# A two-layer hybrid mixer with experts: layer 1's S5 matrices computed during layer 0's experts

## The chip, the cores and the metric

One core of a Trainium2 chip. The metric is the device time of one execution in microseconds (us); lower is better. Engines are named as in the profile: PE (TensorE), DVE (VectorE), ACT (ScalarE), POOL (GpSimd), SP (SyncE, which here only issues DMAs).

## The reference

Two layers over 512 latent and 256 context tokens of width 1024, all in float32. A layer is a mixer of four branches (attention, SSD, S5, short convolution) merged by sigmoid gates, then experts with expert choice. The parts that matter here:

```python
def s5_discretise(lam_re, lam_im, log_step, b_re, b_im):
    step = jnp.exp(log_step)[:, None]
    mag = jnp.exp(lam_re * step)
    ab_re, ab_im = mag * jnp.cos(lam_im * step), mag * jnp.sin(lam_im * step)
    ...
    return ab_re, ab_im, bb_re, bb_im

h[t] = ab * h[t-1] + bb @ u[t]          # complex, 24 groups, both directions
y = re(c @ h) + d * u                   # then gelu and a gate

aff = softmax(h @ w_router); gval, idx = top_k(aff.T, cap)   # cap = 2*T/16
hid = silu(xg @ w_gate) * (xg @ w_up);  ye = (hid @ w_down) * gval
out = zeros.at[idx].add(ye)             # 16 experts, 64 latent and 32 context rows each
```

Layer 1 needs no context output, so only its latents pass the second half of the mixer and the experts. The S5 parameters do not depend on the tokens: the matrices that S5 needs (`ab`'s powers, `bb`, `c`) can be computed at any time.

## The kernel before

Dense products of the mixer are done as three fp32r matmuls (`mm3`, L98 to L100) with operands split by a cast on ACT (L113) and a subtraction on DVE (L114). Tile's scheduler decides the static order of each engine from the program's order and its priorities; no order is written out by hand.

`branches` (L380) emits SSD, S5 and attention, each with its own PSUM tag (a, b, a), and then `main()`: short convolution and 16 `gate` chunks (L409 to L419), which use PSUM tag mm and are the work that PE takes while a branch has nothing for it. In layer 0 they cover 768 tokens (tiles of 512 and 256 columns), in layer 1 the 512 latents.

`s5` (L1002) projects and transposes u, then makes on DVE the step, the exponentials and sines, the powers `pw`, `un`, `lo`, `hi` and the tables `PB`, `PC` (L1023 to L1116). Then it loops over 6 groups of 4 S5 groups. In each: `Bx` by a complex product on POOL (`cmul`, L995 to L1000, called at L1127), `Cx` by a complex product on DVE (L1128; six operations of 128x640), transposes of Bx to `Bt` (L1134), 16 small matmuls for the kernel `KK` (L1143) with its copies (L1147 to L1149) and 8 DMAs on SP that spread KK to `T0` (L1152); then u's transposes, the copy U on ACT (L1158) and the reversed copies Ur on DVE (L1159, L1160), the drive matmuls (L1165, L1166), T by a complex product on POOL (L1172), the rotation by T on DVE (L1177 to L1182), eight scans (L1185), the rotation back to S (L1192 to L1196), the output matmuls (L1201, L1203) and their sum into u_tok (L1207). All of it uses PSUM tag b with three buffers.

`moe` (L1244) runs 16 experts. Per expert `up` (L1340) does the gate product and then the up product for the latents (64 columns, two parts of 512) and the context (32 columns, four parts of 256); `hidden` (L1351) does tanh on ACT (L1357), two DVE operations (L1358, L1359), transposes on PE (L1362) and the copy hidT on ACT (L1364); `down` (L1367) the down product (L1376), the scaling on DVE (L1381) and an indirect DMA on POOL that adds the rows to DRAM (L1384). Expert weights stream on SP in chunks of 1 MB (`wchunks`, L298) through a rotation of buffers. The residual's SBUF tile `x` is idle in that time; it is reloaded at expert 11 (context) and 13 (latents), L1386 to L1388. In layer 0 nothing ties the latent job's matmuls to the context job's: the scheduler may alternate them.

Of the kernel before, what the change touches and what calls it, by code (L numbers as in the profile page):

```python
# [55 lines left out]
MOE = ((2, 3, 3), (3, 3, 2))  # L56


class Kern:
    def __init__(self, ctx, tc, I, out):  # L60
        self.ctx, self.tc, self.nc, self.I, self.out = ctx, tc, tc.nc, I, out
        self.uid = 0
        self.early, self.wafter = (2, 7), {}
# [81 lines left out]
    def setup(self):  # L145
# [30 lines left out]
        self.gs = [dr(f"gs{b}", 8, 128, 768) for b in range(4)]  # L176

# [823 lines left out]

    def s5(self):  # L1002
# [20 lines left out]
        keep = lambda nm, *s: wp.tile([128, *s], F32, name=nm)  # L1023
        bb = [keep("bbr", 25, 16), keep("bbi", 25, 16)]
        cc = keep("cc", 2, 24, 16)
        s5d = keep("s5d", 384)
        PB, PC = keep("PB", 2, 8, 24), keep("PC", 2, 10, 24)
        rho = keep("rho", 24)
        lo, hi = keep("lo", 2, 17, 24), keep("hi", 2, 6, 24)
        with self.pool("s5p") as pp:  # L1030
            sm = lambda nm, *s: pp.tile([128, *(s or (24,))], F32, name=nm)
            p5 = sm("p5", NPS5 - 384)
            nc.scalar.dma_start(p5, self.I["ps5"][l, :, 384:])
            nc.scalar.dma_start(s5d, self.I["ps5"][l, :, :384])
            pr = {k: p5[:, a - 384:b - 384] for k, (a, b) in _PS5.items()}
            V.tensor_copy(cc[:, 0], v3(pr["cr"]))
            V.tensor_copy(cc[:, 1], v3(pr["ci"]))

            step, mag, ang = sm("step"), sm("mag"), sm("ang")
            nc.scalar.activation(step, pr["ls"], AF.Exp)  # L1040
            V.tensor_mul(mag, pr["lr"], step)
            nc.scalar.activation(mag, mag, AF.Exp)
            V.tensor_mul(ang, pr["li"], step)
            t, sn, cn = sm("t"), sm("sn"), sm("cn")
            M = 12582912.0
            V.tensor_scalar(t, ang, 1.0 / (2 * np.pi), M, op0=OP.mult, op1=OP.add)
            V.tensor_scalar(t, t, M, None, op0=OP.subtract)
            V.scalar_tensor_tensor(ang, t, -6.28125, ang, op0=OP.mult, op1=OP.add)
            V.scalar_tensor_tensor(ang, t, -(2 * np.pi - 6.28125), ang, op0=OP.mult, op1=OP.add)
            V.tensor_scalar(ang, ang, 3.1415925, -3.1415925, op0=OP.min, op1=OP.max)  # L1050
            nc.scalar.activation(sn, ang, AF.Sin)
            nc.scalar.activation(cn, ang, AF.Sin, scale=0.5)
            V.tensor_mul(cn, cn, cn)
            V.tensor_scalar(cn, cn, -2.0, 1.0, op0=OP.mult, op1=OP.add)
            pw = sm("pw", 2, 9, 24)
            x1 = sm("x1", 8, 24)
            V.memset(pw[:, 0, 0], 1.0)
            V.memset(pw[:, 1, 0], 0.0)
            V.tensor_mul(pw[:, 0, 1], mag, cn)
            V.tensor_mul(pw[:, 1, 1], mag, sn)  # L1060

            def powers(P, first, last):

                a = 1
                while a < last:
                    n = min(a, last - a)
                    A = [P[:, i, a:a + 1].to_broadcast([128, n, 24]) for i in range(2)]
                    B = [P[:, i, 1:1 + n] for i in range(2)]
                    self.cmul(V, P[:, 0, a + 1:a + 1 + n], P[:, 1, a + 1:a + 1 + n], *A, *B, x1[:, :n])
                    a *= 2  # L1070

            powers(pw, 1, 8)

            nr, den, cr, ci = sm("nr"), sm("den"), sm("cr"), sm("ci")
            ni = pw[:, 1, 1]
            V.tensor_scalar(nr, pw[:, 0, 1], -1.0, None, op0=OP.add)
            V.tensor_mul(den, pr["lr"], pr["lr"])
            V.tensor_mul(t, pr["li"], pr["li"])
            V.tensor_add(den, den, t)
            V.reciprocal(den, den)  # L1080
            V.tensor_mul(cr, nr, pr["lr"])
            V.tensor_mul(t, ni, pr["li"])
            V.tensor_add(cr, cr, t)
            V.tensor_mul(cr, cr, den)
            V.tensor_mul(ci, ni, pr["lr"])
            V.tensor_mul(t, nr, pr["li"])
            V.tensor_sub(ci, ci, t)
            V.tensor_mul(ci, ci, den)
            bc = lambda a: a[:, :, None].to_broadcast([128, 24, 16])
            for b in bb:  # L1090
                V.memset(b[:, 24], 0.0)
            self.cmul(V, bb[0][:, :24], bb[1][:, :24], bc(cr), bc(ci), v3(pr["br"]), v3(pr["bi"]), sm("y1", 24, 16))

            V.memset(PC, 0.0)
            for s in range(8):
                V.tensor_copy(PB[0:64, :, s], pw[0:64, :, 7 - s])
            V.tensor_copy(PB[64:128], pw[64:128, :, 0:8])
            V.tensor_copy(PC[0:64, :, 0:9], pw[0:64])
            for k in range(9):
                V.tensor_copy(PC[64:128, :, 9 - k], pw[64:128, :, k])  # L1100

            V.tensor_mul(rho, mag, mag)
            V.tensor_mul(rho, rho, rho)
            V.tensor_mul(rho, rho, rho)
            un = sm("un", 2, 9, 24)
            V.tensor_copy(un[:, 0, 1], cn)
            V.tensor_copy(un[:, 1, 1], sn)
            for a in (1, 2, 4):
                A = [un[:, i, a:a + 1] for i in range(2)]
                self.cmul(V, un[:, 0, 2 * a:2 * a + 1], un[:, 1, 2 * a:2 * a + 1], *A, *A, x1[:, :1])  # L1110
            V.memset(hi[:, 0, 0], 1.0)
            V.memset(hi[:, 1, 0], 0.0)
            V.tensor_copy(lo[:, :, 1], un[:, :, 8])
            powers(lo, 1, 16)
            V.tensor_copy(hi[:, :, 1], lo[:, :, 16])
            powers(hi, 1, 5)  # L1116
        with self.pool("s5b") as bp:
            W = lambda nm, *s: bp.tile([128, *s], F32, name=nm)
            for g0 in range(0, 24, 4):
                gg = slice(g0, g0 + 4)  # L1120

                Bx = [W(f"Bx{i}", 4, 8, 16) for i in range(2)]
                Cx = [W(f"Cx{i}", 4, 10, 16) for i in range(2)]
                z1, e1 = W("z1", 4, 10, 16), W("e1", 4, 8, 16)
                ap = lambda P, n, i: P[:, i, :, gg].rearrange("p s g -> p g s")[:, :, :, None].to_broadcast([128, 4, n, 16])
                av = lambda v, n: v[:, gg][:, :, None, :].to_broadcast([128, 4, n, 16])
                self.cmul(nc.gpsimd, Bx[0], Bx[1], ap(PB, 8, 0), ap(PB, 8, 1), av(bb[0], 8), av(bb[1], 8), e1)  # L1127
                self.cmul(V, Cx[0], Cx[1], ap(PC, 10, 0), ap(PC, 10, 1), av(cc[:, 0], 10), av(cc[:, 1], 10), z1)  # L1128
                nc.scalar.mul(Cx[1], Cx[1], -1.0)
                Bt = [W(f"Bt{i}", 4, 128) for i in range(2)]  # L1130
                for i in range(2):
                    ps = self.va(512)
                    for q in range(4):
                        nc.tensor.transpose(ps[:, q * 128:(q + 1) * 128], Bx[i][:, q].rearrange("p s i -> p (s i)"), self.ident)  # L1134
                    nc.scalar.copy(Bt[i].rearrange("p a b -> p (a b)"), ps)

                KK = bp.tile([16, 4, 15, 16], F32, name="KK")
                kf = [self.va(128).rearrange("p (d j) -> p d j", d=8) for _ in range(2)]
# [15 lines left out]
                U, Ur = W("U", 4, 96), W("Ur", 4, 96)  # L1154
                ps = self.va(384).rearrange("p (g b) -> p g b", g=4)
                for q in range(4):
                    nc.tensor.transpose(ps[:, q], u_tok[:, g0 + q].rearrange("p s i -> p (s i)"), self.ident[:96, :96])
# [3 lines left out]
                pv = []  # L1161
                for i in range(2):
                    p = self.va(384).rearrange("p (g b) -> p g b", g=4)
                    for q in range(4):
                        nc.tensor.matmul(p[0:64, q], Bt[i][:, q, 0:64], U[:, q], start=True, stop=True, skip_group_check=True)  # L1165
                        nc.tensor.matmul(p[64:128, q], Bt[i][:, q, 64:128], Ur[:, q], start=True, stop=True, skip_group_check=True)  # L1166
                    pv.append(p)
# [91 lines left out]
    def experts(self, l, mp, slotT, io, m5):  # L1259
# [3 lines left out]
        with self.pool("gat", side="right") as gp, self.pool("exp", side="right") as wp, ExitStack() as es:  # L1263
# [76 lines left out]
            def up(w, X, ps, job, e, side):  # L1340
# [3 lines left out]
                for k in range(8):  # L1344
# [3 lines left out]
                    if k % 4 == 3:  # L1348
                        next(side, None)
# [301 lines left out]
```

## Time and profile before

| | |
|---|---|
| runs (3) | 3120.9 to 3125.51 us, median 3123.74 |
| profiled execution | 3125.83 us, span 3124.1 us, mean granted clock 0.966 |
| PE busy | 2846.2 us (91%) |
| DVE / ACT / POOL busy | 1559.2 / 783.8 / 619.7 us |
| layer 0's S5 | about 360 to 546 us of the span |
| layer 0's experts | 1131.6 to 1732.9 us |
| layer 1's S5 | about 2004 to 2242 us, its gates go on until about 2440 |

The span is one execution as the profiler recorded it; the profiled execution's own time is 1.7 us more. Line numbers are those of the kernel before.

### The profile page before, as it was taken

To read this page: it belongs to the slowest core of one execution; us is meant where nothing else is said; L and a number is where in the kernel's file an instruction comes from. 1 tells how busy PE (TensorE), PEld (TensorE's weight loads), DVE (VectorE), ACT (ScalarE), POOL (GpSimd) and SP (SyncE) were. 2 spreads that over 40 slices of the span, in tenths; PEclk is the share of its full clock that TensorE was granted. 3 is DMA by queue.
4 is the path that set the end of the run, shared out by engine and by line. 5 is a ranking of instruction groups with operands and counts; after the bars stand their busy time and mean duration, and the time that the engine had idled before them with its cause. 6 is when DMAs were issued, how large, how long until landed. Compare 5 with 4: busy or idle time off the path is not lost. (4 is left out here: it accounts for less than half of the span.)

```text
span 3124.1 us, 47057 instructions
## 1 busy us (share of the span) xinstructions
PE 2846.2 (91%) x18626; PEld 1826.3 (58%) x18626; DVE 1559.2 (50%) x3507; ACT 783.8 (25%) x1725; POOL 619.7 (20%) x765
## 2 busy tenths in 40 slices
PE   7999878999999979999999799977999896998887
PEld 4866756788888943433333376756687684332223
DVE  5477688555436552212111546798856565232223
ACT  4253222426522200000000332322436421000001
POOL 1022165120004121111110104065220031010001
PEclk9999999999999989999999899988999997999999
DMA  7324424311256479999996531432320486999998
GB/s 234 116 69 132 139 89 124 120 48 53 79 199 200 155 278 396 402 383 351 339 363 254 183 110 54 153 105 75 98 76 25 162 283 254 409 408 409 409 409 305
DMA packets 323039, 659.79 MB, mean 211 GB/s; under 512 B 22017, under 2 KB 191233, under 8 KB 322818
## 3 DMA queue, kind: packets, MB, share of 16 engines
q1 hardware_dynamic: 300688, 601.66, 53.6%
q10 hardware_dynamic: 15186, 32.93, 2.8%
q0 software_dynamic: 6944, 22.19, 2.3%
q8 instruction: 147, 2.41, 0.3%
q14 instruction: 74, 0.61, 0.1%
HBM read 602.85 MB, written 50.71 MB: 209 GB/s over the span
## 5 line engine op out<-in xcount | busy, mean ns | idle before, releaser
L1346 PE MATMUL psa<-we,X 128*64 128x512 f32 (+1 forms) x4096 | 605.1, 494 | 31.2 <-DMA we<-in_w_exp_gate_dram 15.8
L1346 PEld LDWEIGHTS psa<-we,X 128*64 128x64 f32 (+1 forms) x4096 | 193.7, 123 | 422.9 <-issue 318.7
L98 PE MATMUL psmm<-hH,fwH 128*128 128x512 f32 x984 | 374.1, 380 | 7.8 <-DVE xpad L636 3.6
L100 PE MATMUL psmm<-hH,fwL 128*128 128x512 f32 x984 | 368.3, 374 | 0.0
L99 PE MATMUL psmm<-hL,fwH 128*128 128x512 f32 x984 | 368.2, 374 | 0.0
L1376 PE MATMUL psa<-we,hidT 128*64 128x512 f32 x992 | 248.7, 609 | 21.3 <-ACT hidT L1364 14.9
L98 PEld LDWEIGHTS psmm<-hH,fwH 128*128 128x128 f32 x984 | 190.8, 194 | 51.4 <-issue 14.6
L1357 ACT ACTIVATE hid<-psa 128x512 f32<-128x512 f32 (+1 forms) x48 | 25.3, 526 | 779.1 <-PE psa L1346 739.3
L100 PEld LDWEIGHTS psmm<-hH,fwL 128*128 128x128 f32 x984 | 190.6, 194 | 30.7 <-issue 5.9
L99 PEld LDWEIGHTS psmm<-hL,fwH 128*128 128x128 f32 x984 | 191.1, 194 | 29.2 <-issue 6.1
L1381 DVE SCALAR_TENSOR_TENSOR y<-psa,ag,m 64x512 f32<-64x512 f32 x62 | 46.5, 750 | 274.0 <-PE psa L1376 273.4
L1376 PEld LDWEIGHTS psa<-we,hidT 128*64 128x64 f32 x992 | 67.8, 138 | 156.9 <-issue 112.5
L1359 DVE TENSOR_TENSOR hid<-hid,psa 128x512 f32<-128x512 f32 (+1 forms) x48 | 28.7, 597 | 252.1 <-PE psa L1346 251.8
L114 DVE TENSOR_TENSOR fwL<-fr,fwH 128x1024 fp32r<-128x1024 f32 (+1 forms) x100 | 117.1, 1172 | 73.4 <-ACT fwH L113 64.6
L471 POOL TENSOR_TENSOR merged<-merged,tgm 128x512 f32<-128x512 f32 (+1 forms) x48 | 62.8, 1326 | 424.0 <-DVE tgm L469 423.7
L1337 POOL TENSOR_TENSOR X<-X,modT 128x512 f32<-128x512 f32 x40 | 42.4, 1073 | 491.3 <-DVE X L1336 474.9
L1358 DVE SCALAR_TENSOR_TENSOR hid<-hid,psa 128x512 f32<-128x512 f32 (+1 forms) x48 | 28.7, 598 | 221.8 <-ACT hid L1357 221.8
L98 PE MATMUL psa<-cwH,hH 128*128 128x256 f32 (+1 forms) x432 | 122.1, 283 | 0.1
L113 ACT CAST fwH<-fr 128x1024 fp32r<-128x1024 f32 (+1 forms) x100 | 89.6, 897 | 128.2 <-DMA fr<-in_w_in_dram 62.1
L100 PE MATMUL psa<-cwH,hL 128*128 128x256 f32 (+1 forms) x432 | 121.6, 282 | 0.0
L99 PE MATMUL psa<-cwL,hH 128*128 128x256 f32 (+1 forms) x432 | 121.3, 281 | 0.0
L416 ACT ACTIVATE tg<-psmm 128x512 f32<-128x512 f32 x96 | 51.2, 533 | 160.4 <-PE psmm L100 152.8
(528 smaller groups left out, 5879.1 us busy)
## 6 DMA issues: line engine op xcount, KB each, us to landing
we<-in_w_exp_gate_dram SPq DMA_DIRECT2D x128, 1024.0 KB
we<-in_w_exp_up_dram SPq DMA_DIRECT2D x128, 1024.0 KB
we<-in_w_exp_down_dram SPq DMA_DIRECT2D x128, 1024.0 KB
fr<-in_w_mod_dram SPq DMA_DIRECT2D x96, 512.0 KB
fr<-in_w_in_dram SPq DMA_DIRECT2D x64, 512.0 KB
raw<-in_w_in_dram SPq DMA_DIRECT2D x36, 512.0 KB
gs<-tg ACTq DMA_DIRECT2D x32, 384.0 KB
tgm<-gs SPq DMA_DIRECT2D x32, 384.0 KB
```

Source lines behind the costliest of these rows:

```text
L98: self.nc.tensor.matmul(ps, ah, bh, start=start and i == 0, stop=False)
L99: self.nc.tensor.matmul(ps, ah, bl, start=False, stop=False)
L100: self.nc.tensor.matmul(ps, al, bh, start=False, stop=stop and i == n - 1)
L113: self.nc.scalar.copy(h, x)
L114: self.nc.vector.tensor_sub(l, x, h.bitcast(F32))
L416: nc.scalar.activation(tg[:, o:o + n], self.cm(w, m, o, n), AF.Tanh, scale=0.5)
L471: (V if i == 3 else nc.gpsimd).tensor_add(dst, dst, t)
L1337: nc.gpsimd.tensor_add(X[:, hk], X[:, hk], Bm[:, 24 + h * 4:28 + h * 4, s:s + 1].to_broadcast([128, 4, 128]))
L1346: self.lastup = nc.tensor.matmul(ps[s][j * c:(j + 1) * c], X[s][:, k, r:r + c], w(k)[:, j * n:(j + 1) * n], start=k == 0, stop=k == 7, ski ...
L1358: V.scalar_tensor_tensor(hid, hid, 1.0, g, op0=OP.add, op1=OP.mult)
L1376: nc.tensor.matmul(ps[j * c:(j + 1) * c], lh, w(k)[:, j * n:(j + 1) * n], start=k == 0, stop=k == 7, skip_group_check=True)
L1381: V.scalar_tensor_tensor(Y[s][r, nn], ps[j * c:(j + 1) * c], got[s][1][r, e:e + 1], m5[s][r, nn], op0=OP.mult, op1=OP.mult)
```

## The change

`s5_params` is a generator that makes layer 1's Bt, Cx, T0 and T during layer 0's experts, in the tile x and one small extra tile, and writes them to DRAM (`s5w`, 6 groups of 128x3328, 10.2 MB; rho to `s5r`) by DMAs on ACT's queue. `advance` runs it one step further three times per expert: between the gate and the up products (untied), after `hidden` (each DVE operation tied behind `lasthid`, the last hid product of the program's order, the context's) and after `down` (tied behind `lasty`, the last scaled rows). The `yield`s set the calendar: expert 0 exponentials and sines, 1 powers, 2 and 3 T (3 groups each), 4 the tables, 5 to 11 one S5 group per expert in three steps (B behind lasthid; Bx's transposes and C behind lasty; kf, KK and 8 DMAs between the next expert's gate and up). Layer 1's `s5` then only loads rho and, per group, one tile `mt` on SP.

In both layers the loop is pipelined: the drive of the next group is emitted before the scans of this one, its matrices after the output matmuls; the Ur copies go from DVE to ACT, read from PSUM; transposes, kf and outputs move to PSUM tag a. In layer 0's experts the order of the products is fixed by dependencies: gate latents, gate context, up context, up latents, and down latents before down context. Layer 0's PSUM split among the tags a, b, mm changes as the first line of the diff shows, and x is reloaded as a whole at expert 13.

```diff
-MOE = ((2, 3, 3), (3, 3, 2))
+MOE = ((4, 2, 2), (3, 3, 2))
...
+    class Behind:                 # wraps an engine
...
+                if self.k.order is not None:
+                    self.k.tc.add_manual_dep(ins.ins, self.k.order.ins.name,
+                                             mybir.DependencyInfo(mybir.DependencyClass.NoSync, mybir.DependencyReason.DATA))
...
+    def s5_params(self, l, x, pool):
+        V, Q = self.Behind(self, nc.vector), nc.scalar
+        out = self.s5w
...
+        for c in range(6):
+            self.cmul(V, T[0], T[1], h4(0), h4(1), l4(0), l4(1), at(E1, 4, 6, 16))
+            Q.dma_start(out[c][:, 2560:], buf[:, :768])
+            if c % 3 == 2:
+                yield
+                yield
+                yield
...
+        for c in range(6):
+            self.cmul(V, bb[0][:, :4], bb[1][:, :4], bc(cr), bc(ci), br[:, gg], bi[:, gg], at(E1, 4, 16))
+            self.cmul(V, Bx[0], Bx[1], ap(PB, 8, 0), ap(PB, 8, 1), av(bb[0][:, :4], 8), av(bb[1][:, :4], 8), at(E1, 4, 8, 16))
+            yield
+            for i in range(2):
+                ps = self.pa(512)
+                for q in range(4):
+                    nc.tensor.transpose(ps[:, q * 128:(q + 1) * 128], Bx[i][:, q].rearrange("p s i -> p (s i)"), self.ident)
+                nc.scalar.copy(Bt[:, i].rearrange("p a b -> p (a b)"), ps)
+            Q.dma_start(out[c][:, 0:1024], OUT)
+            self.cmul(V, Cx[0], Cx[1], ap(PC, 10, 0), ap(PC, 10, 1), av(cc[0][:, gg], 10), av(cc[1][:, gg], 10), at(E1, 4, 10, 16))
+            nc.scalar.mul(Cx[1], Cx[1], -1.0)
+            for i in range(2):
+                Q.dma_start(out[c][:, 1024 + 512 * i:1536 + 512 * i].rearrange("p (g s j) -> p g (s j)", g=4, s=8),
+                            Cx[i][:, :, 1:9].rearrange("p g s j -> p g (s j)"))
+            yield
...
+            for s in range(8):
+                Q.dma_start(out[c][s * 16:(s + 1) * 16, 2048:2560].rearrange("p (g d) -> p g d", g=4),
+                            KK[:, :, 7 - s:15 - s].rearrange("p g d j -> p g (d j)"))
+            yield
+
+    def advance(self, after=None):
+        self.order = after
+        next(self.ahead, None)
+        self.order = None
...
+            def drive(g0):
+                if l == 0:
...
+                else:
+                    mt = bp.tile([128, self.S5W], F32, name="mt", bufs=2)
+                    nc.sync.dma_start(mt, self.s5w[g0 // 4])
...
+                nc.scalar.copy(U, ps)
+                nc.scalar.copy(Ur[:, :, 0:32], ps[:, :, 31::-1])
+                nc.scalar.copy(Ur[:, :, 32:96], ps[:, :, 95:31:-1])
...
-                nc.scalar.copy(U, ps)
-                V.tensor_copy(Ur[:, :, 0:32], U[:, :, 31::-1])
-                V.tensor_copy(Ur[:, :, 32:96], U[:, :, 95:31:-1])
...
+            nxt, mats = drive(0), matrices(0)
+            for g0 in range(0, 24, 4):
+                (U, pv), (Cx, T0, T) = nxt, mats
...
+                if g0 < 20:
+                    nxt = drive(g0 + 4)
                 for i in range(2):
                     for q in range(4):
                         V.tensor_tensor_scan(...)
...
+                if g0 < 20:
+                    mats = matrices(g0 + 4)
...
-                    for job in jobs:
-                        up(wg, X, pg, job, e, side)
+                    turns = [(wg, pg, job) for job in jobs]
                     wu = wtile()
-                    for job in jobs:
-                        up(wu, X, pu, job, e, side)
+                    turns += [(wu, pu, job) for job in jobs[::-1]]
+                    for i, (w, p, job) in enumerate(turns):
+                        up(w, X, p, job, e, side, self.lastup if i and both else None)
+                        if i == 1:
+                            self.advance()
...
                 hids = hidden(pg, pu)
+                self.advance(self.lasthid)
...
                 down(e, hids, got, Y)
+                self.advance(self.lasty)
+                if both and e == 13:
+                    for t in self.tiles:
+                        nc.gpsimd.dma_start(x[:, t - self.tiles[0]], self.home(t))
```

PE in a late expert of layer 0, before (we: a weight chunk, X: the gathered tokens, 64x512 a latent matmul, 32x256 a context one):

```order
L1346 MATMUL psa<-we,X_14310 64x512 x4
L1346 MATMUL psa<-we,X_14340 32x256 x8
L1346 MATMUL psa<-we,X_14310 64x512 x4
L1346 MATMUL psa<-we,X_14340 32x256 x9
L1346 MATMUL psa<-we,X_14310 64x512 x4
L1362 MATMUL psb<-cst,hid_14740 128x128 x4
L1376 MATMUL psa<-we,hidT_14749 64x512 x3
```

and with the change, from the end of one expert to the end of the next one's up product:

```order
L1596 MATMUL psb<-cst,hid_14061 128x128 x2
L1610 MATMUL psa<-we,hidT_14059 64x512 x16
L1610 MATMUL psb<-we,hidT_14068 32x256 x32
L1161 MATMUL psmm<-cst,x 128x128 x8
L1578 MATMUL psa<-we,X_13758 64x512 x16
L1578 MATMUL psa<-we,X_13792 32x256 x32
L1179 MATMUL psmm<-x 32x128 x16
L1578 MATMUL psa<-we,X_13792 32x256 x32
L1578 MATMUL psa<-we,X_13758 64x512 x16
```

The jobs alternate every four to nine matmuls before; with the change each product runs through, the latents' up product comes last, and the moved transposes (L1161) and kf matmuls (L1179) stand between products.

DVE in expert 5 with the change (hid_13145 latents, hid_13156 context; x: the moved step, here B of the first group):

```order
L1592 SCALAR_TENSOR_TENSOR hid_13145<-hid_13145,psa 128x512
L1592 SCALAR_TENSOR_TENSOR hid_13156<-hid_13156,psa 128x256
L1593 TENSOR_TENSOR hid_13156<-hid_13156,psa 128x256
L1017 TENSOR_TENSOR x<-x 128x64 x5
L1017 TENSOR_TENSOR x<-x 128x512
L1017 TENSOR_TENSOR x<-x 128x64
L1017 TENSOR_TENSOR x<-x 128x512 x5
L1593 TENSOR_TENSOR hid_13145<-hid_13145,psa 128x512
```

The step stands behind the context's product and ahead of the latents' one, on which the next transposes wait. ACT in the next expert (DMA s5w x8: the spread of KK):

```order
L1591 ACTIVATE hid_13453<-psa 128x512
L1183 COPY x<-psmm 16x128 x4
L1185 COPY x<-psmm 16x112 x4
L1187 DMA s5w<-x 16x4x128 x8
L1591 ACTIVATE hid_13464<-psa 128x256
L1598 COPY hidT_13462<-psb 128x512
```

Eight copies and eight DMA issues stand between the latents' tanh and the context's.

DVE in layer 1's S5, before, from the end of one group to the rotation of the next (z, Cx: the complex product; fwL: a weight split):

```order
L1196 TENSOR_TENSOR S_17483<-g_17466,g_17467 64x4x64
L996 TENSOR_TENSOR z_17517<-PC,cc 128x640
L114 TENSOR_TENSOR fwL<-fr,fwH 128x1024
L1207 TENSOR_TENSOR u_tok<-u_tok,psb 96x512
L995 TENSOR_TENSOR Cx_17515<-PC,cc 128x640
L998 TENSOR_TENSOR Cx_17516<-PC,cc 128x640
L997 TENSOR_TENSOR Cx_17515<-Cx_17515,z_17517 128x640
L999 TENSOR_TENSOR z_17517<-PC,cc 128x640
L1000 TENSOR_TENSOR Cx_17516<-Cx_17516,z_17517 128x640
L114 TENSOR_TENSOR fwL<-fr,fwH 128x1024
L1159 COPY Ur<-U 128x4x32
L1160 COPY Ur<-U 128x4x64
```

and with the change:

```order
L1420 TENSOR_TENSOR S_17970<-g_17923,g_17924 64x4x64
L1399 TENSOR_TENSOR Vr_18000<-mt,psb 128x384
L1400 TENSOR_TENSOR g_18002<-mt,psb 128x384
L115 TENSOR_TENSOR fwL<-fr,fwH 128x1024
L1401 TENSOR_TENSOR Vr_18000<-Vr_18000,g_18002 128x384
L1433 TENSOR_TENSOR u_tok<-u_tok,psa 96x512
```

The complex product and the Ur copies are gone, and the next group's rotation follows at once on the last group's S.

## Rows read from the trace of the kernel before

**Rows 1.** The page: busy us by engine, share of the span, instructions.

```profile
PE 2846.2 (91%) x18626; PEld 1826.3 (58%) x18626; DVE 1559.2 (50%) x3507; ACT 783.8 (25%) x1725; POOL 619.7 (20%) x765
```

**Rows 2.** Stretches: us, busy PE, PEld, DVE, ACT, POOL, PEclk, DMA share, GB/s.

```profile
360.00:546.00 186.00, 152.74 (x1148) 115.85 (x1148) 163.57 (x312) 45.50 (x102) 111.80 (x102) 0.91 0.36 110
2004.00:2060.00 56.00, 50.16 (x307) 40.50 (x305) 43.91 (x162) 15.64 (x25) 11.60 (x13) 1.00 0.44 142
2060.00:2120.00 60.00, 47.44 (x308) 32.95 (x308) 53.54 (x82) 16.17 (x34) 40.47 (x32) 0.86 0.33 98
2120.00:2180.00 60.00, 48.51 (x311) 37.68 (x312) 47.71 (x73) 15.71 (x33) 35.85 (x32) 0.86 0.22 65
2180.00:2242.00 62.00, 52.39 (x356) 40.83 (x356) 54.84 (x89) 19.76 (x38) 27.35 (x27) 0.94 0.32 93
2242.00:2440.00 198.00, 195.73 (x1265) 158.36 (x1264) 120.07 (x337) 97.65 (x238) 20.78 (x56) 1.00 0.18 59
```

**Rows 3.** PE's longest wait, 2004 to 2242 (us in total, times, longest).

```profile
PE psb L1166 <- DVE Ur L1160: 13.4, 6, 4.5
```

**Rows 4.** DVE's groups, 2004 to 2242 (count, busy us, mean ns).

```profile
L114 DVE TENSOR_TENSOR fwL<-fr,fwH 128x1024 fp32r<-128x1024 f32 x19 | 30.7, 1614 | 8.0 <-ACT fwH L113 7.8
L1185 DVE TENSOR_TENSOR_SCAN Vr<-rho,Vr 128x96 f32<-128x96 f32 x48 | 13.4, 341 | 0.0
L996 DVE TENSOR_TENSOR z<-PC,cc 128x640 f32<-128x640 f32 x6 | 9.8, 1640 | 0.2
...
L1207 DVE TENSOR_TENSOR u_tok<-u_tok,psb 96x512 f32<-96x512 f32 x6 | 4.1, 676 | 1.3 <-PE psb L1203 1.3
...
L1177 DVE TENSOR_TENSOR Vr<-Tr,psb 128x384 f32<-128x384 f32 x6 | 3.3, 550 | 8.6 <-PE psb L1166 8.6
```

**Rows 5.** Single lines over the whole span (ns, min/median/max).

```profile
L996 DVE TENSOR_TENSOR z<-PC,cc x12: 806/1652/1733, 383.3 to 2214.8; 128x640 f32<-128x640 f32 x12
L1159 DVE COPY Ur<-U x12: 213/1133/1283, 391.5 to 2224.2; 128x128 f32<-128x128 f32 x12
L1160 DVE COPY Ur<-U x12: 278/281/1368, 392.3 to 2224.3; 128x256 f32<-128x256 f32 x12
```
```profile
L1152 SPq DMA_DIRECT2D T<-KK x96: 585/593/1294, 396.7 to 2234.5; - x96
```

**Rows 6.** PE's timeline in layer 1's S5: two gate matmuls, Bx's transposes.

```profile
2113.12 0.39 PE L98 MATMUL psmm<-hH,fwH 128*128 128x512 f32 x1
2113.36 0.39 PE L99 MATMUL psmm<-hL,fwH 128*128 128x512 f32 x1
```
```profile
2123.35 1.04 PE L1134 MATMUL psb<-cst,Bx 128*128 128x128 f32 x8
```

**Rows 7.** PE's wait in layer 0's S5, 360 to 546.

```profile
PE psb L1166 <- DVE Ur L1160: 13.8, 5, 4.5
```

**Rows 8.** Stretches of layer 0's experts: number 1; numbers 0 to 14.

```profile
1172.30:1206.90 34.60, 34.20 (x301) 13.68 (x297) 7.71 (x17) 1.94 (x4) 6.90 (x6) 1.00 1.03 399
```
```profile
1131.60:1694.70 563.10, 556.25 (x4509) 199.99 (x4509) 115.23 (x242) 29.11 (x60) 88.57 (x89) 1.00 0.97 369
```

**Rows 9.** PE's timeline: expert 1's start and latents' down product; starts of 14 and 6.

```profile
1172.34 21.29 PE L1346 MATMUL psa<-we,X 128*64 128x512 f32 x192
...
1196.31 7.08 PE L1376 MATMUL psa<-we,hidT 128*64 128x512 f32 x30
...
1656.67 23.50 PE L1346 MATMUL psa<-we,X 128*64 128x512 f32 x192
```
```profile
1346.94 3.65 PE L1346 MATMUL psa<-we,X 128*64 128x512 f32 x15
```

**Rows 10.** DVE's timeline: the latents' product of expert 1; layer 1's S5 parameters.

```profile
1190.08 0.69 DVE L1359 TENSOR_TENSOR hid<-hid,psa 128x512 f32<-128x512 f32 x1 [9.29 <-PE psa L1346]
```
```profile
2023.29 0.18 DVE L1041 TENSOR_TENSOR mag<-p,step 128x24 f32<-128x24 f32 x1
...
2028.00 0.20 DVE L999 TENSOR_TENSOR x<-pw 128x48 f32<-128x48 f32 x1
```

More of the change, by code (lines that the diff above doesn't have):

```diff
@@ L62, in __init__ @@
         self.uid = 0
+        self.ahead = iter(())
         self.early, self.wafter = (2, 7), {}
@@ L1022, in s5 @@
                                       ps.rearrange("p s (g i) -> p s g i", g=8))
[L1023 to L1033, printed above, removed]
-            nc.scalar.dma_start(s5d, self.I["ps5"][l, :, :384])
[L1035 to L1116, printed above, removed]
@@ L1117, in s5 @@
         with self.pool("s5b") as bp:
             W = lambda nm, *s: bp.tile([128, *s], F32, name=nm)
[L1119 removed]
+            av = lambda v, n, gg: v[:, gg][:, :, None, :].to_broadcast([128, 4, n, 16])
+            ap = lambda P, n, i, gg: P[:, i, :, gg].rearrange("p s g -> p g s")[:, :, :, None].to_broadcast([128, 4, n, 16])
+            def drive(g0):
                 gg = slice(g0, g0 + 4)
[L1122 removed]
+                if l == 0:
+                    Bx = [W(f"Bx{i}", 4, 8, 16) for i in range(2)]
+                    e1 = W("e1", 4, 8, 16)
+                    self.cmul(nc.gpsimd, Bx[0], Bx[1], ap(PB, 8, 0, gg), ap(PB, 8, 1, gg), av(bb[0], 8, gg), av(bb[1], 8, gg), e1)
+                else:
+                    mt = bp.tile([128, self.S5W], F32, name="mt", bufs=2)
+                    nc.sync.dma_start(mt, self.s5w[g0 // 4])
+                    self.mt[g0] = mt
+                U, Ur = bp.tile([128, 4, 96], F32, name="U", bufs=2), W("Ur", 4, 96)
+                ps = self.va(384, "a").rearrange("p (g b) -> p g b", g=4)
+                for q in range(4):
+                    nc.tensor.transpose(ps[:, q], u_tok[:, g0 + q].rearrange("p s i -> p (s i)"), self.ident[:96, :96])
+                nc.scalar.copy(U, ps)
+                nc.scalar.copy(Ur[:, :, 0:32], ps[:, :, 31::-1])
+                nc.scalar.copy(Ur[:, :, 32:96], ps[:, :, 95:31:-1])
+                if l == 0:
+                    Bt = [W(f"Bt{i}", 4, 128) for i in range(2)]
+                    for i in range(2):
+                        ps = self.va(512, "a")
+                        for q in range(4):
+                            nc.tensor.transpose(ps[:, q * 128:(q + 1) * 128], Bx[i][:, q].rearrange("p s i -> p (s i)"), self.ident)
+                        nc.scalar.copy(Bt[i].rearrange("p a b -> p (a b)"), ps)
+                else:
+                    Bt = [mt[:, i * 512:i * 512 + 512].rearrange("p (q c) -> p q c", q=4) for i in range(2)]
+                pv = []
+                for i in range(2):
+                    p = self.va(384).rearrange("p (g b) -> p g b", g=4)
+                    for q in range(4):
+                        nc.tensor.matmul(p[0:64, q], Bt[i][:, q, 0:64], U[:, q], start=True, stop=True, skip_group_check=True)
+                        nc.tensor.matmul(p[64:128, q], Bt[i][:, q, 64:128], Ur[:, q], start=True, stop=True, skip_group_check=True)
+                    pv.append(p)
+                return U, pv
@@ L1126, in s5 @@
-                av = lambda v, n: v[:, gg][:, :, None, :].to_broadcast([128, 4, n, 16])
-                self.cmul(nc.gpsimd, Bx[0], Bx[1], ap(PB, 8, 0), ap(PB, 8, 1), av(bb[0], 8), av(bb[1], 8), e1)
-                self.cmul(V, Cx[0], Cx[1], ap(PC, 10, 0), ap(PC, 10, 1), av(cc[:, 0], 10), av(cc[:, 1], 10), z1)
-                nc.scalar.mul(Cx[1], Cx[1], -1.0)
[L1130 to L1135, printed above, removed]
+                T = [W(f"Tr{i}", 4, 6, 16) for i in range(2)]
@@ L1137, in s5 @@
                 KK = bp.tile([16, 4, 15, 16], F32, name="KK")
-                kf = [self.va(128).rearrange("p (d j) -> p d j", d=8) for _ in range(2)]
+                kf = [self.va(128, "a").rearrange("p (d j) -> p d j", d=8) for _ in range(2)]
                 for d in range(2):
@@ L1263, in experts @@
         with self.pool("gat", side="right") as gp, self.pool("exp", side="right") as wp, ExitStack() as es:
+            if both:
+                self.ahead = self.s5_params(1, x, es.enter_context(self.pool("s5x", side="right")))
             self.weB = [es.enter_context(self.pool("weB", b)) for b in self.lay[l]]
@@ L1338, in rows, with behind, up @@
                 return X
-            def up(w, X, ps, job, e, side):
+            def behind(ins, first):
+                tc.add_manual_dep(ins.ins, first.ins.name, mybir.DependencyInfo(mybir.DependencyClass.NoSync, mybir.DependencyReason.DATA))
+            def up(w, X, ps, job, e, side, first=None):
                 s, c, parts, o = job
@@ L1347, in up @@
                                          skip_group_check=True)
+                        if first is not None and k + j == 0:
+                            behind(self.lastup, first)
                     if k % 4 == 3:
@@ L1375, in down @@
                         for j in range(parts):
-                            nc.tensor.matmul(ps[j * c:(j + 1) * c], lh, w(k)[:, j * n:(j + 1) * n], start=k == 0, stop=k == 7,
-                                             skip_group_check=True)
+                            ins = nc.tensor.matmul(ps[j * c:(j + 1) * c], lh, w(k)[:, j * n:(j + 1) * n], start=k == 0, stop=k == 7,
+                                                   skip_group_check=True)
+                            if s and k + j == 0:
+                                behind(ins, last_)
+                    last_ = ins
                     r = slice(e * c % 128, e * c % 128 + c)
```

264 lines of the change are left out of this document (239 added, 25 removed).

## The prediction

> **What bounds the kernel now.** The page first: PE is busy for most of the span, no other engine for more than half of it [rows 1]. So whatever shortens the kernel must either take work from PE or fill the places where PE idles or runs below full clock. This change takes none: it has as many PE instructions as before. The second view, busy time by stretch, shows where PE loses [rows 2]. In layer 1's S5 stage, 2004 to 2242, busy time times granted clock is 50.2 + 40.8 + 41.7 + 49.2 = 181.9 us of work at full clock in 238 us: 56.1 us are lost. Right behind it, 2242 to 2440, PE works 195.7 of 198 us at clock 1.00 on the gates that were left over. In the S5 stage DVE is the busy one: 53.5 of 60 us where the clock is lowest. (A granted clock of 1.00 is the level of 2.4 GHz; 0.86 is a mean over that and stretches at 1.2 GHz.) The waits name the link: S5's drive matmuls wait for the Ur copies on DVE [rows 3]. Layer 0's S5 looks alike (DVE 163.6 of 186 us [rows 2], the same wait 13.8 us [rows 7]). The experts are another regime: PE has hardly a gap and the DMA engines are as full as they get, share 1.03 at 399 GB/s in expert 1 [rows 8].
>
> **Layer 1's S5 stage.** Removed from DVE: all parameters, six 128x640 operations per group, the Ur copies; from POOL: both complex products; from PE: transposes and kf. What DVE still does in a group: six rotations at 0.55 and eight scans at 0.341 [rows 4]; rotating back, four operations of the rotations' size at 0.55 and six smaller ones, which I count as four of the same (2.2); the sum into u_tok and the share of weight splits, some 2.3 (one operation of 0.7, and one split of 1.61 [rows 4]; 19 splits stood in the stage, but 204 gate matmuls instead of 489 stay in it, so about 8 of them for 6 groups). Together 3.3 + 2.7 + 4.4 + 2.3 = 12.7, for six groups 76 us, and about 20 for u's projection and its transposes ahead of them: a floor of 96. PE's work in the stage: 181.9, less the 285 gate matmuls that the new order puts behind the stage, at 0.235 us from one to the next [rows 6] 67, less the moved work. That is one set of Bx transposes, 1.04 us [rows 6], and 16 kf matmuls, which I put at the same, so 2.1 a group, 12 in all (11 inside the stretch). 104 us stay, above DVE's floor. How well will they run? At the 0.90 of the first stretch, where POOL hardly works (50.2 of 56), 116 us; at the 0.69 of the two worst stretches 151 [rows 2]. I take 0.87, 120 us, nearer the first row because POOL's products and DVE's parameters are gone, a little below it because less filler is left. The moved gates cost 68 behind the stage, at the 0.99 of the row from 2242. 120 + 68 = 188 against 238: **−50**. Ends: −67 (all that is lost comes back, and the moved work) and −19 (0.69: 151 + 68).
>
> The loads of mt, 1.7 MB a group on SP, are new: 10.2 MB at a DMA share of 0.22 to 0.44 [rows 2], two tiles ahead; I cost them at nothing, the free share covers them, and if a tile came late a group's rotation would wait for it.
>
> **Layer 0's S5 stage.** Here only the Ur copies leave DVE: medians 1.133 + 0.281 us, six times [rows 5], 8.5 us of an engine that is busy nearly throughout. ACT takes them at 45.5 busy of 186 [rows 2]. **−9.** Ends: −16, if the pipelined order also takes away all 13.8 us of the wait [rows 7] and a little more; +3, if the reordering only moves waits. The shortest copies are 0.213 and 0.278, so alone they are worth 0.49 x 6 = 3. The Trainium skill ("SBUF — State Buffer", section "Who interferes with whom") says that DVE and GpSimd share a port pair, held by one of them for a whole instruction. By that rule a long copy waits for a POOL product, and the next operation on DVE would wait for it in its place: the sum would have −3 instead of −9. The row of the complex product on DVE agrees, 0.806 against a median of 1.652 [rows 5].
>
> **Layer 0's experts.** Experts 1 to 5 run their products one after the other, 34.92 us each (1172.34 to 1346.94); 6 to 14 alternate the jobs, (1694.7 − 1346.94) / 9 = 38.64, the gate and up products alone 23.50 instead of 21.29 [rows 8, 9]. The fixed order gives ten experts (15 too) 3.7 us each: −37. Against it:
> - the moved matmuls, on the path here: 6 x 2.1 = +13;
> - the latents' up product is now last, so its DVE product, 0.69, which now ends under the context's matmuls [rows 10], is open in 15 experts: +10;
> - steps ahead of that product. They start when the context's product is done, and the latents' up product covers 7.1 us (the latents' down product, of the same size, takes that [rows 9]). Powers: 46 small operations at 0.12 ((2028.00 − 2023.29) / 39 [rows 10]) 5.6, covered; T: 13 at about 0.5, covered; tables 51 and wider copies, 7 to 9: +2;
> - five experts carry a spread of KK and a step B. Eight copies on ACT (about 2 us), eight issues at 0.593 as on SP's queue [rows 5] 4.7, then tanh and two products for the context (1.2), then B, six 128x512 and small ones, about 5: 13 against 3.7 + 7.1 of cover: 2, rounded down to 1.2 because issues may be cheaper on ACT: +6.
>
> Sum −37 + 13 + 10 + 2 + 6 = **−6**. The DMA queue sets another floor: 563.1 us at 369 GB/s are 208 MB [rows 8]; 11.0 MB come on top (10.2 written, 0.8 read), and 219 MB at 399 GB/s are 548 us, so no more than −15. Other end: the added bytes at that rate are 28 us, and if they came wholly on top of PE's sum, +22.
>
> **Sum.** −50 − 9 − 6 = −65. The profiled execution took 3125.8, so 3060.8; the median of the runs is 2.1 lower: **3059 us**. All else I leave at nothing: the reload of x at one expert instead of two, since it lands long before the mixer reads it, and PSUM's new split.
>
> **Rivals.**
> - *The S5 stage stays a chain.* Pipelining only overlaps neighbours; if each group still goes drive, rotation, scan, output in turn, PE's clock stays at the worst rows' 0.69: −19 − 9 − 6 = −34, 3090. For it: fewer gate matmuls are left to fill. Against: on DVE the next rotation now stands right behind S.
> - *The experts are paced by the weight stream.* The share of 1.03 [rows 8] says that no DMA engine is free while expert 1 runs; then the 11 MB cost all their time: −50 − 9 + 22 = −37, 3087. Against: the share is 0.97 over the stage, at 369 GB/s. The Trainium skill ("DMA: Bandwidth & Descriptors", section "Issuing engines are not separate DMA queues") says that DMAs issued by ACT run on the same 16 engines as SP's; so writing through ACT's queue would not save the stream from them.
> - *Slower: in-order queues of ACT and DVE.* If issues cost 1.294 (the longest [rows 5]) and the steps run at the rate beside POOL, 1.65 [rows 5], each of the five experts waits 2 + 10.4 + 1.2 + 10.5 − 10.8 = 13 us, 67 in all instead of 6, and the T experts 13 x 1.65 − 7.1 = 14 twice: −65 + 61 + 28 = +24, 3148. It decides from about 13 us a step in each of those experts on. Against: POOL is busy only 6.9 of 34.6 us there [rows 8].
> - *It does not do what it says:* the next group's drive stands behind this group's outputs on some engine, and the tied steps give the experts back what they gained: within 6 us of before.
>
> **How the numbers follow.** 0.2%, about 6 us, is what a measurement of this kernel can tell from no change. Forecast 0.62, the chain 0.15, the stream 0.15, in-order queues 0.05, no effect 0.03. The first three are faster: 0.92; same 0.03; slower 0.05. The range: down to all best ends, −67 − 16 − 15 = −98, 3026, rounded to 3025; up past both faster rivals, 3100; that leaves out the last two rivals and a case with both faster ones at once.
>
> **What would show it.** Layer 1's S5 outputs should follow within about 120 us of its first transposes at a clock and busy share near 0.87 together, and the gates end about 50 us earlier relative to them; POOL nearly idle there; no wait of drive matmuls for Ur on DVE in either layer. In the experts: gate and up in one block of about 21.3 us per expert, a wait of the latents' transposes on DVE of 0.7 to 3 us, a DMA share near 1.0. The prediction is wrong if experts 5 to 11 take over 40 us each, if PE waits there for weights, or if S5's stage in layer 1 is still above 150 us.

## The result and the profile after

The changed kernel took 3041.15 us (median of 4 runs, 3032.92 to 3042.54); the kernel before, beside it, 3124.62. Ratio 0.9728, 95% interval 0.9708 to 0.9749: faster, by 83.5 us where 65 were forecast, inside the range. The profiled executions, 3042.23 against 3125.83, differ by 83.6, so their traces can be laid side by side. They show a sum that came out near partly by luck: nearly all of it lies in layer 1.

| stretch, us of the span, by landmarks of both traces | before | after | forecast | measured |
|---|---|---|---|---|
| start to the last gate of layer 0 | 898.7 | 898.0 | -9 | -1 |
| first matmul of layer 0's experts to their last | 1131.7 to 1732.9 | 1131.3 to 1733.7 | -6 | +1 |
| start of layer 1's last gate activation | 2445.1 | 2385.1 | -50 | -60 |
| start of the last POOL sum of layer 1's merge | 2526.4 | 2442.7 | 0 | -84 in all, 24 of it behind the gates |

Layer 1, by stretch of the changed kernel (us, busy PE, PEld, DVE, ACT, POOL, granted clock, DMA share, GB/s): S5, the gates behind it in two pieces, and from the last gate to the merge's last sum; then layer 0's S5.

```profile
2004.00:2106.00 102.00, 95.64 (x730) 74.86 (x729) 80.47 (x179) 22.91 (x44) 11.32 (x30) 1.00 0.64 221
2106.00:2250.00 144.00, 141.74 (x870) 114.60 (x869) 88.44 (x261) 66.62 (x145) 20.73 (x56) 1.00 0.23 70
2250.00:2385.00 135.00, 134.85 (x811) 107.01 (x810) 56.53 (x114) 63.19 (x153) 0.00 (x0) 1.00 0.35 115
2385.10:2442.70 57.60, 56.93 (x249) 46.84 (x250) 36.91 (x47) 18.38 (x24) 23.71 (x15) 1.00 0.71 227
360.00:546.00 186.00, 151.84 (x1156) 113.46 (x1155) 162.16 (x303) 47.79 (x112) 108.23 (x101) 0.90 0.34 106
```

S5's stage takes 102 us instead of 238 and the clock stays at its upper level, 2.4 GHz, where it averaged 0.86 to 0.94 for three quarters of the stage [rows 2]. About the stretch from the last gate to the merge's end in the kernel before:

```profile
2440.00:2526.40 86.40, 76.29 (x381) 60.06 (x378) 47.62 (x71) 31.25 (x57) 23.83 (x15) 0.94 0.65 218
```

There the last attention heads ran behind the gates (their outputs leave until 2458.0), PE then waited 6.6 us, and the merge's first product started at 2464.2, 19 us after the last gate; at a clock of 0.80 from 2458 to 2475 its first matmuls took 0.63 us instead of 0.39. After, attention is done at 2322.5, under the gates that S5 left over; the merge starts 0.7 us after the last gate, and PE loses less than a microsecond in the tail. Layer 0's S5 line is what it was [rows 2].

In layer 0's experts the longest of PE's waits is now for the hid product (PE's waits, 1165 to 1735; us in total, times, longest):

```profile
PE psb L1596 <- DVE hid L1593: 27.7, 14, 6.8
PE psa L1578 <- DMA we<-in_w_exp_up_dram: 1.9, 4, 0.9
```

What stands ahead of that product in expert 2 is T (DVE's timeline, start, us), and this is PE meanwhile:

```profile
1221.45 0.42 DVE L1593 TENSOR_TENSOR hid<-hid,psa 128x256 f32<-128x256 f32 x1
1221.79 11.86 DVE L1017 TENSOR_TENSOR x<-x 128x384 f32<-128x384 f32 x13
1233.57 0.68 DVE L1593 TENSOR_TENSOR hid<-hid,psa 128x512 f32<-128x512 f32 x1
```
```profile
1206.38 21.15 PE L1578 MATMUL psa<-we,X 128*64 128x512 f32 x192
1234.30 1.54 PE L1596 MATMUL psb<-cst,hid 128*128 128x128 f32 x6 [5.76 <-DVE hid L1593]
1236.15 8.41 PE L1610 MATMUL psa<-we,hidT 128*64 128x512 f32 x32 [0.30 <-ACT hidT L1598]
```

The products run in one block of 21.15 us, as forecast. But 13 operations take 11.86 us, 0.91 each on average, where about 0.5 was put in. The average mixes two kinds: a product of T's views takes 1.1 us, a sum of contiguous results 0.55 (the first and the fourth operation):

```profile
1221.79 1.11 DVE L1017 TENSOR_TENSOR x<-x 128x384 f32<-128x384 f32 x1
```
```profile
1224.86 0.55 DVE L1017 TENSOR_TENSOR x<-x 128x384 f32<-128x384 f32 x1
```

POOL has nothing to do from 1210.1 to 1246.4, so it does not slow them. PE waits 5.76 us, and after the wait the next products run slower for a while (8.41 instead of 7.1 us, granted clock 0.92 over the expert). Expert 2 takes 41.7 us, expert 3 44.3. In expert 7 the eight issues for KK hold the context's tanh (ACT's timeline):

```profile
1411.68 8.52 ACTq L1187 DMA_DIRECT2D s5w<-x  x8
1420.24 0.38 ACT L1591 ACTIVATE hid<-psa 128x256 f32<-128x256 f32 x1 [8.38 <-DMA s5w<-x]
```

Of these 8.52 us the issues themselves take 3.7; 4.5 are a pause before the fifth, which waits for an earlier DMA to s5w.

### The profile page after: what moved, and what is told of

Its sections match the earlier page's. It is cut to its first block, busy times and chain, and to the rows that moved or that the text cites. A ratio compares the mean times of both kernels' runs of the same rounds, so it can differ in the third digit from the quotient of the medians.

```text
span 3040.5 us, 47083 instructions
## 1 busy us (share of the span) xinstructions
PE 2771.3 (91%) x18626; PEld 1817.4 (60%) x18626; DVE 1561.6 (51%) x3583; ACT 786.6 (26%) x1749; POOL 518.7 (17%) x693
## 3 DMA queue, kind: packets, MB, share of 16 engines
q10 hardware_dynamic: 27666, 43.19, 3.9%
## 5 line engine op out<-in xcount | busy, mean ns | idle before, releaser
L1578 PE MATMUL psa<-we,X 128*64 128x512 f32 (+1 forms) x4096 | 583.9, 491 | 37.0 <-DMA we<-in_w_exp_gate_dram 18.7
L1578 PEld LDWEIGHTS psa<-we,X 128*64 128x64 f32 (+1 forms) x4096 | 203.5, 123 | 391.6 <-issue 273.1
L1610 PE MATMUL psa<-we,hidT 128*64 128x512 f32 x992 | 234.4, 610 | 18.6 <-ACT hidT L1598 13.0
L115 DVE TENSOR_TENSOR fwL<-fr,fwH 128x1024 fp32r<-128x1024 f32 (+1 forms) x100 | 109.0, 1091 | 101.1 <-ACT fwH L114 91.8
L1565 POOL TENSOR_TENSOR X<-X,modT 128x512 f32<-128x512 f32 x40 | 42.9, 1083 | 521.8 <-DVE X L1564 452.8
```

The source lines that it names most:

```text
L115: self.nc.vector.tensor_sub(l, x, h.bitcast(F32))
L1565: nc.gpsimd.tensor_add(X[:, hk], X[:, hk], Bm[:, 24 + h * 4:28 + h * 4, s:s + 1].to_broadcast([128, 4, 128]))
L1578: self.lastup = nc.tensor.matmul(ps[s][j * c:(j + 1) * c], X[s][:, k, r:r + c], w(k)[:, j * n:(j + 1) * n], start=k == 0, stop=k == 7, ski ...
L1610: ins = nc.tensor.matmul(ps[j * c:(j + 1) * c], lh, w(k)[:, j * n:(j + 1) * n], start=k == 0, stop=k == 7, skip_group_check=True)
```

## The experiments

The theory after the result: layer 1 gained because its S5 no longer has DVE and POOL work; in the experts the order gained and the moved steps ate it. Each run was measured beside the kernel before (its medians 3122 to 3125), and its ratio is to that. "E1-15" is the time from the end of the first expert's context down product to that of the last one's, from PE's timeline of one profiled execution: 560.4 us before, 562.0 after. Kernels with the same experts agree in it: 521.0, 521.0 and 521.1 with the order alone, untied bytes and in place, 562.0 and 562.9 in the changed kernel and inline. The diffs of this section are shortened and put in words where they are long.

**Order alone; and the bytes alone, twice.**

```diff
 (the kernel before)
+MOE[0] = (4, 2, 2); fixed order of gate, up and down products as in the change
 (bytes alone: and, in experts 5 to 10)
+nc.scalar.dma_start(self.s5w[e - 5], xf[:, :3328])          # first run: untied
+behind(that DMA, last hidT copy of the expert)              # second run
```

> The kernel before with only the fixed order of the experts' products and the PSUM split 4, 2, 2; no S5 work is moved. Theory (PE paces the experts; in the changed kernel the moved steps ate what the order gained): the alternation goes, -37, the latents' hid product is open, +10, so about -27 or 3098 us, and the experts end near 1706 instead of 1733 of the span. Rival (the weight stream paces the experts, so no order helps): no more than -15, 3110 us or above. Rival 2 (the order gains nothing because the down products cost what the up products save): within 6 us of before.

> The order alone, and in experts 5 to 10 one DMA each on ACT's queue that writes 1.7 MB of the idle residual tile to DRAM: the bytes of the moved matrices without any of their work (what is written is used by nothing). Theory (the stream has room): within 6 us of the order alone. Rival (the stream paces the experts): 10.2 MB at 399 GB/s, about +26 us on the order alone.

> The earlier run with the bytes alone had put its six DMAs ahead of the experts (1112 to 1150 of the span), where they delayed the first one. Here each is tied behind the hidT copy of experts 5 to 10. Theory now (the fixed order already runs at the stream's limit, share 1.03, so bytes cost their time): the experts 20 to 26 us longer than with the order alone, some 3100 to 3110 us. Rival (room in the stream; the changed kernel's experts are slow from PE's waits and moved matmuls alone): within 6 us of the order alone, 3084 us.

Order alone: 3083.75 us, ratio 0.9876 (0.9858 to 0.9893), E1-15 521.0: the order is worth 39 us, more than any of the theories said (the profiled execution, 3074.89, was the fastest of the four, so E1-15 is compared here and not the spans). The PSUM split changed with it; no run takes the two apart. Untied bytes: 3097.02, ratio 0.992 (0.9902 to 0.9938), but E1-15 again 521.0; the DMAs had run ahead of the experts, so this run says nothing on the question. Tied bytes: 3090.28, ratio 0.9893 (0.9876 to 0.9909), E1-15 526.8, with PE waiting 4.9 us for weights: the theory of this run missed. The 26 us of a stream without room are excluded; about 6 us are what the bytes cost in whole rows (the intervals of the two times overlap; the 6 us rest on E1-15).

```profile
1167.30:1688.40 521.10, 505.40 (x4497) 207.90 (x4493) 115.08 (x218) 28.86 (x62) 75.83 (x75) 1.00 0.98 376
```
```profile
1172.20:1699.00 526.80, 506.23 (x4493) 207.43 (x4493) 115.07 (x218) 28.87 (x62) 75.86 (x75) 1.00 1.00 391
```

Experts 1 to 15 of the order alone, and with tied bytes (columns as above): at a DMA share of 0.98 the stream still had room for 15 GB/s.

**The steps off PE's path.**

```diff
 (the changed kernel, context's up product last)
-turns += [(wu, pu, job) for job in jobs[::-1]]
+turns += [(wu, pu, job) for job in jobs]
 (KK late: also, KK's eight DMAs one step later)
+add_manual_dep(each of them, last hidT copy)
 (behind the latents' product: the changed kernel with)
-self.lasthid = V.tensor_mul(hid, hid, u)
+ins = V.tensor_mul(hid, hid, u); if s == 0: self.lasthid = ins
-            if c % 3 == 2: yield; yield; yield
+            yield
```

> The changed kernel with one difference: the context's up product comes last instead of the latents'. The latents' hid product then ends under it, and the tied steps start behind everything that PE waits for in the expert. Theory (steps on PE's path): the T experts lose their 17 us of surplus, the hid product's 0.8 us in 15 experts goes (12 us), the S5 experts lose some 10 of their surplus; limited by the stream, whose share is 0.96 there already: 15 to 27 us below the changed kernel, 3014 to 3026 us. Rival (the stream alone sets the pace now): within 6 us of the changed kernel.

> As the kernel with the context last, and the eight DMA issues of KK's spread stand behind the expert's last hidT copy on ACT instead of ahead of the context's tanh. Theory: PE's waits for hid in experts 6 to 11 go, 5 to 10 us below the kernel with the context last, about 3010 to 3018 us. Rival (the stream paces): no difference from it.

> The changed kernel with the steps tied behind the latents' hid product (the one that ends last on PE) instead of the context's, and T made one group per step instead of three. Theory (steps ahead of that product cost 16 us in the T experts and some 10 in the S5 experts; the stream allows 13 at most): 8 to 15 us faster than the changed kernel, 3026 to 3033 us. Rival (the stream takes all of it): within 6 us of the changed kernel.

> As the kernel with the steps behind the latents' product, and KK's eight DMA issues stand behind the expert's last hidT copy on ACT. Theory (the issues delay the context's tanh, but the steps no longer hang on it): within 4 us of the former. Rival (the issues themselves hold hidT): 5 to 10 us faster than it.

Context last: 3041.34, ratio 0.9742 (0.9722 to 0.9762), E1-15 560.8: no gain, a miss. No expert waits for hid any more, but an expert without a step is 0.64 us longer than in the order alone (34.6 against 33.9), one T expert still takes 42.9, with a wait of 4.6 for the X product that now stands behind T on DVE, and PE waits 6.6 us for weights. KK late on top: 3045.01, ratio 0.9754 (0.9736 to 0.9772), no gain, a miss too. Steps behind the latents' product: **3028.37, ratio 0.9694 (0.9677 to 0.971)**, E1-15 552.0, 13 us less than the changed kernel and as expected. The two intervals just touch (0.971 and 0.9708); the ratios differ by 0.0034, their half-widths together (root of the sum of squares) give 0.0026. KK late on top of it: 3035.78, 0.9719 (0.9702 to 0.9735), no gain either: 7 us more, where within 4 was expected, with overlapping intervals.

By expert (PE's timeline, us; one execution each, that of the last column the slowest of its four), the gain of the steps behind the latents' product lies with T alone:

| | order alone | changed | context last | behind the latents' |
|---|---|---|---|---|
| experts 2 and 3 (T) | 70.2 | 86.0 | 77.5 | 72.2 |
| experts 5 to 12 (S5 groups) | 281.1 | 303.7 | 309.6 | 308.9 |

So the wait behind T was real and could be had back. In the experts with S5 groups the waits for hid (10.3 us from 1326 to 1600) shrank too, but the experts became no shorter: waits for weights stand in their place. Moving ACT's issues gained nothing in either place. What is left in the kernel with the steps behind the latents' product, PE's waits:

```profile
PE psa L1575 <- DMA we<-in_w_exp_up_dram: 11.1, 8, 2.9
PE psb L1595 <- DVE hid L1590: 8.2, 12, 0.8
```

**Packets.** The copy of Cx to DRAM in whole rows:

```diff
-Q.dma_start(out[c][:, 1024 + 512 * i:...], Cx[i][:, :, 1:9])   # pieces of 512 bytes
+Q.dma_start(out[c][:, 1024 + 640 * i:1664 + 640 * i], (B0, B1)[i][:, :640])
```

> As the kernel with the steps behind the latents' product, but Cx goes to DRAM as it lies in SBUF, ten steps of 16 in one row of 2560 bytes per partition and matrix, instead of eight steps picked out in pieces of 512 bytes: 4608 packets fewer, 0.8 MB more. Theory (PE now waits 11 us for weights in the S5 experts because short packets take the DMA engines' time out of proportion): 4 to 10 us faster than that kernel, 3018 to 3024 us. Rival (bytes count, not packets): no faster, 3028 us or up to 3 more.

3025.52, ratio 0.9683 (0.9666 to 0.9699), E1-15 545.1, waits for weights 8.2 instead of 11.1 us. Lowest of all, but its interval and that of the kernel it is compared with overlap: not shown as a gain. The other kernel's profiled execution was the slowest of its four (3035.94), which makes the 7 us of E1-15 look larger than they may be.

**Order taken out of the change.** MOE and the products as before, all else as changed.

> The changed kernel without the fixed order of the experts' products and with the PSUM split of before; the moved steps and their ties stay. Theory (order gives 39 us alone, and the steps' 41 come on top of whatever the order is): 25 to 40 us slower than the changed kernel, 3066 to 3081 us. Rival (with the steps in, the stream is the limit, and order is worth nothing more): within 10 us of the changed kernel.

3064.89, ratio 0.9821 (0.9805 to 0.9838), E1-15 581.8: 24 us slower than the changed kernel (20 by E1-15), just short of what was expected. Order is worth 39 us without the moved steps and 20 to 24 with them.

**What in layer 1 made the gain.**

```diff
 (in place: the changed kernel, moved work off)
-            if both: self.ahead = self.s5_params(...)
-        if l == 1:   # in s5: load from DRAM
+        if False:   # and the branches that hang on it
 (inline: the changed kernel, in s5's loop)
+                if l == 1: nxt, mats = drive(g0), matrices(g0)
```

> The changed kernel without the moved work: layer 1 makes its S5 matrices itself, as layer 0 does, in the pipelined loop with the Ur copies on ACT; the experts keep their fixed order. Theory (what freed layer 1's S5 was taking the parameters and complex products off DVE and POOL): layer 1 gains only 0 to 20 of its 84 us; with the experts as in the order alone some 3080 to 3100 us. Rival (pipelining and the Ur copies made the gain): layer 1 keeps at least 60 of the 84 us, and with the experts' order the kernel is at 3035 us or below.

> The changed kernel with layer 1's S5 loop not pipelined: each group's drive and matrices are emitted at the start of its own turn; the matrices still come from DRAM and Ur from ACT. Theory (removal of work is what counts; DVE's in-order queue holds only short operations and gate matmuls fill PE): 0 to 20 us slower than the changed kernel, 3041 to 3061 us. Rival (the chain drive, rotation, scans, outputs sets the stage, and pipelining broke it): 40 us or more slower, 3081 us or above.

In place: 3078.54, ratio 0.985 (0.9831 to 0.987), a little below what was expected and far from the rival's 3035. Inline: 3048.41, ratio 0.9755 (0.9733 to 0.9777), as expected. Layer 1's S5 from u's first transposes to the last output, in place, inline, in this order:

```profile
1957.00:2196.70 239.70, 203.98 (x1294) 156.46 (x1293) 199.25 (x401) 72.59 (x145) 113.30 (x102) 0.91 0.36 109
```
```profile
1997.30:2112.50 115.20, 106.56 (x775) 84.10 (x773) 84.94 (x183) 24.71 (x45) 12.44 (x30) 0.99 0.60 206
```

In place it lasts 239.7 us, as with the order alone (240.7) and little less than before (244.8); the changed kernel has 110.1 between the same landmarks. The tail from the last gate to the merge's last sum is back too: 81.0 us, 81.3 before. So pipelining and the Ur copies on ACT are worth next to nothing while DVE is busy 199 of 240 us: 5 us in the medians against the order alone, with overlapping intervals. Inline the stage lasts 115.2 against 110.1, and the median is 7 us higher, again with overlapping intervals: with the work gone, pipelining gives 7 us at most that a median shows. The moved work is the gain. How much of it is due to DVE's part, POOL's or PE's, no run takes apart.

## Why the prediction was right or wrong

**Layer 1, right in mechanism, too small.** The chain of reasons held: the work moved off DVE, POOL and PE was the cause, PE's loss in the stage came back, the gates ran behind it at full clock, the mt tiles came in time (no wait for them shows). Three sizes were off. The stage took 102 us and not 120: PE's work in it was 95.6 us at full clock instead of 104 (which part of that sum was too high stays open), and the step "I take 0.87" was too low, 0.94, above the first stretch's 0.90; each makes about 9 us. The stretch behind it to the last gate grew by 76 us (203 to 279), not 68. The traces show 438 gate matmuls in the stage before and 168 after, so 270 moved and not 285, some 63 us at the forecast's 0.235; the other 12 or so, by difference, are the attention that had come after the last gate. And the step "all else I leave at nothing" missed the tail: the gates moved behind S5 cover attention's last heads, 24 us. With -60 and -24 layer 1 gave more than the upper end of its term, -67, because that end counted the S5 stretch alone.

**Layer 0's S5, wrong.** -9 came from the Ur copies' medians times six. The wait for Ur [rows 7] is gone, but PE is busy 151.8 us of 186 at clock 0.90, as before [rows 2]. PE's waits in 360 to 570 come to 33.5 us before and 33.7 after. One of the larger ones stood there already (first line, before) and shrank; the others took Ur's place:

```profile
PE psmm L208 <- DVE modT L203: 13.5, 3, 5.2
```
```profile
PE psmm L212 <- DVE modT L207: 8.8, 3, 5.1
PE psa L1379 <- DVE Cx L1001: 7.4, 3, 3.2
PE psa L1345 <- ACT KK L1385: 6.6, 3, 5.1
PE psa L1345 <- POOL Bx L1001: 4.2, 1, 4.2
```

DVE's complex product, POOL's, and ACT's copies of KK remained; DVE is busy 162.2 us instead of 163.6. The step that failed is that a copy's median on a crowded DVE is time that removal gives back. By the rule of the Trainium skill that the prediction names ("SBUF — State Buffer", "Who interferes with whom") the term would have been -3, nearer to the -1 measured; that the next operation waits in the copy's place fits DVE's busy time, but no run here took the ports apart.

**The experts, wrong in both terms, near in the sum by luck.** Order: -37 + 10 was forecast, -39 came (560.4 to 521.0). The open hid product is there, 0.8 us in an expert, 9.9 in all. Even so experts 6 to 15 gave 37 us (386 to 349), and 1 to 5, which had no alternation to lose, 2.7 more. In expert 1 the gate and up products take 21.15 us instead of 21.29, and from the first transposes to the end of the latents' down product it is 9.3 instead of 9.8, since the context's transposes no longer break into that product. So the 34.92 us of experts 1 to 5, from which the gain was worked out, was not the floor.

Moved steps: +21 was forecast (13 + 2 + 6), 41 came (521.0 to 562.0): 15.8 in experts 2 and 3, 22.6 in 5 to 12, the rest elsewhere. The moved matmuls are cheaper than forecast, 1.02 + 0.65 us a group in PE's timeline, 10 in all. PE's idle time in experts 1 to 15 grew by 19 us (15.7 to 34.8), its waits for hid from 9.9 to 27.7; the last 12 us, by difference, are products that run slower behind the long waits (mean clock 0.98 instead of 1.00). "T: 13 at about 0.5, covered" is the step that failed most: 0.91 each, experts 2 and 3 together 16 us longer. T's product had run on POOL before, so no row of DVE showed it; the 0.55 came from operations of that size with another operand pattern, and T's own sums do take 0.55, its products 1.1. The rival of ACT's and DVE's in-order queues had the place right (wait of the latents' product behind the step, the issues on ACT) and a price that was too high, as the forecast's was too low; it did not turn the sign, since B's operations took 0.68 us each, not the 1.65 beside POOL. Of experts 5 to 11 two took over 40 us (44.1 and 40.6), their mean was 38.4.

**The stream, settled in part.** Its rival (+28 us) is excluded by the tied bytes, 6 us. The forecast's own floor of the stream, no more than -15, did not hold either: with the 10.2 MB tied in, experts 1 to 15 are 34 us shorter than before (560.4 to 526.8). Yet once the steps are off PE's path PE waits 11 us for weights. The bytes are the same; but ACT's queue has 15186 packets in the whole kernel before, 16050 with the tied bytes and 27666 in the changed kernel: 864 more against 12480 more. Whether packets are the cause stays open: 4608 fewer of them lowered that wait by 3 us and E1-15 by 7, but not the time beyond its interval.

## What to carry to other kernels

Work that starves PE in one stage is worth moving to a stage where DVE is mostly idle, and the gain may go on beyond the stage, since the filler it frees covers the next tail. A step put on an in-order engine belongs behind the product that the busy engine waits for last, not behind the last one in program order: that tie, together with smaller steps, was worth 13 us here, all of it in the experts with T. Where the busy engine then waits for something else, as for weights in the experts with S5 groups, moving the step gains nothing. Price an operation that changes its engine by a row with the same operand pattern, not the same size.

## What the runs showed that was not expected

- A DVE product of two 128x384 views, one broadcast and one run through in steps of 24 floats, took 1.10 to 1.12 us (24 of them in the changed kernel); sums of contiguous operands of that size in the same steps mostly 0.55 to 0.56. Products with broadcast views that are not strided in this way cost as much as the sums beside them: 0.68 to 0.69 (128x512) and 0.80 to 0.83 (128x640). So the strided view is the likely cause; no run changed it alone.
- A DMA share of 1.03 in single experts [rows 8] was not the end: with 10.2 MB more, the fixed order's experts went from 376 to 391 GB/s and lost 6 us, not 26.
- The same DMA issue on ACT took from 309 to 1555 ns in the changed kernel (48 of them, median 437), and in expert 7 a row of eight was stretched by a wait of 4.5 us for an earlier DMA:

```profile
L1187 ACTq DMA_DIRECT2D s5w<-x x48: 309/437/1555, 1376.0 to 1578.3; - x48
```
